# Moving weights laid with even columns first and read by TensorE from two halves in turn

## The chip, the core and the metric

The kernel runs on one core of one Trainium2 chip. The metric is device microseconds of one execution; lower is better. A core has five engines that run side by side, each with its own stream of instructions and synchronised by semaphores: TensorE (PE in the profile, with its weight loads as PEld), VectorE (DVE), ScalarE (ACT), GpSimd (POOL) and SyncE (SP), which here issues the transfers.

A matmul has two operands in on-chip memory (SBUF). The stationary one, 128 by 128, is loaded into the array first (LDWEIGHTS). The moving one is streamed past it, column by column: 128 partitions by up to 512 columns. In this kernel an activation block is stationary in some matmuls and a weight block in others; this change is about matmuls in which the *weight* is the moving operand.

## What is computed

A decoder trunk of two layers on 512 tokens with 1024 channels, all in float32. The parts that matter here, from the reference:

```python
def sq_relu_mlp(h, w_up, w_down):                      # both layers, d_ff = 4096
    u = jnp.matmul(h, w_up)
    return jnp.matmul(jnp.square(jax.nn.relu(u)), w_down)

for layer in range(2):
    h = rms_norm(x, mix_pre_g[layer])
    if layer < 1:
        m = pool_mixer(h, pool_w[layer], pool_scale[layer])
    else:
        q = jnp.matmul(h, w_q[0]) ...
        o = stick_breaking_attention(q, k, v)          # 16 heads of 64
        m = jnp.matmul(o..., w_o[0])
    x = x + rms_norm(m, mix_post_g[layer])
    h = rms_norm(x, mlp_pre_g[layer])
    x = x + rms_norm(sq_relu_mlp(h, w_up[layer], w_down[layer]), mlp_post_g[layer])
    if layer == 0:
        kv = jnp.matmul(rms_norm(x, kv_norm_g), w_kv)  # keys: first 1024 columns, values: last 1024
```

## The kernel before

Tokens lie in four blocks of 128 (`TS`), output channels in two blocks of 512 (`NS`). Float32 products are made from operands split into a high and a low part of type `fp32r`; a product is then three matmuls: high by high, high by low, low by high. The helper `mm3` (lines 317 to 320) emits these three for one pair of blocks, and its three lines carry them in the profile. Operands declared plain `F32` (the pooling mixer's products, line 872, and the scale row, line 802) aren't split by hand: one such matmul of the program shows as two rows in the trace.

Matmuls with the weight as the moving operand:

- `Seven.product`, line 625: the down projection of 28 of the 32 blocks of d_ff in each layer. Seven products stand for eight (a Strassen scheme over pairs of token halves and channel halves), in five groups of 2, 3, 3, 3 and 3 pairs of blocks. VectorE forms sums and differences of the weight's quarters (`right`, lines 592 to 611), ScalarE and VectorE split them into high and low parts (`split`, line 298), and the matmuls read them as `w[:, z, q]`, 512 columns at a time.
- `contract` (line 466), `finish` (line 480) and `projected` inside the attention's `end` (line 1187), all through `mm3`: the attention's output projection and the last four blocks of each down projection. In the last layer's last token block one 512 is cut into two of 256.
- `half_values` (line 941), through `mm3`: the values of the first eight heads, 512 columns wide. The values of the other heads (`values`, line 962) are 256 wide.

The up projection, queries and keys (`up_block`, lines 739 to 753, matmul lines 744, 747 and 748) have the weight stationary and the activations `xnh` and `xnl` moving.

Weights come from device memory by transfers that SP issues; the host lays each array out beforehand (in `kernel`, lines 1346 to 1387). Before the change the moving weights' columns lie in their natural order, so a moving operand of 512 columns is 512 neighbouring 4-byte words of each partition.

The order on each engine is partly written out by hand (`MIX_ORDER`, `ATT_ORDER`, `END_ORDER`, `MLP_ORDER`), and otherwise set by a planner.

Of the kernel before, what the change touches and what calls it, by code (L numbers as in the profile page):

```python
# [15 lines left out]
P = 128  # L16
D = 1024
S = 512
T = S // P
KC = D // P  # L20
FF = 4096
NJ = FF // P
# [6 lines left out]
PAIRS = HEADS // 2  # L29
# [2 lines left out]
TINY = 1e-24  # L32
TS = [slice(t * P, (t + 1) * P) for t in range(T)]
NS = [slice(0, 512), slice(512, 1024)]


SEG = {3: (0, 512), 2: (512, 384), 1: (896, 256), 0: (1152, 128)}
# [73 lines left out]
def trunk(ctx, tc, x, bands, grow, pw, wup, wdn, wq, wk, wv, wo, out):  # L111
# [16 lines left out]
    def ps():  # L128
        return psum.tile([P, 512], F32, tag="ps", name=name("ps"))
# [5 lines left out]
    ident, gc = eye[:, :P], eye[:, P:]  # L135
    for n in NS:
        nc.sync.dma_start(xt[0][:, n], x[TS[0], n])
# [7 lines left out]
    def xn_tile():  # L145
        turn[0] += 1
        return xn3[:, turn[0] % 3]
# [65 lines left out]
    apart, kept, going = [], {}, []  # L213
# [40 lines left out]
    def fill(n=1):  # L254
        if gate[0]:
            behind.update(latest)
        for _ in range(n):
            if queue and len(made) < ahead and (queue[0][0][0] != "dn" or dn_pool[0]):
                make()

    def get(key):
        while key not in made:
            make()
        return made.pop(key)

    for l in range(2):
        if l == 1:
            n = len(queue)
# [48 lines left out]
    def mm3(dst, ah, al, bh, bl, start, stop):  # L317
        nc.tensor.matmul(dst, ah, bh, start=start, stop=False)  # L318
        nc.tensor.matmul(dst, ah, bl, start=False, stop=False)  # L319
        nc.tensor.matmul(dst, al, bh, start=False, stop=stop)  # L320

    xnh = keep.tile([P, KC, S], F32R, tag="xnh", name="xnh")
    xnl = keep.tile([P, KC, S], F32R, tag="xnl", name="xnl")
# [6 lines left out]
    class Update:  # L330
        def __init__(self, t, gpost, scaled, eps=EPS, gpre=None, final=False, xn=None, gcol=None):
# [7 lines left out]

            self.cuts = NS  # L340
            if final and t == T - 1:
                self.cuts, self.scaled = [NS[0], slice(512, 768), slice(768, 1024)], xn_tile()

# [5 lines left out]
        def product(self, n, y, within=False):  # L349

            cut = self.cuts[n]
            if within:
                self.held[n] = y
            out = y if within else self.scaled[:, cut]
            return nc.vector.tensor_tensor(out=out, in0=y, in1=self.gpost[:, cut], op=ALU.mult)
# [110 lines left out]
    def contract(lhs, w, y, first, tiles):  # L466
        last = len(lhs) - 1
        for t in tiles:
            for n in NS:
                pd = ps()  # L470
                for c, ((lh, ll), (wh, wl)) in enumerate(zip(lhs, w)):
                    mm3(pd, lh[:, TS[t]], ll[:, TS[t]], wh[:, n], wl[:, n], c == 0, c == last)
                part = y[t][:, n]
                if first:
                    nc.scalar.copy(part, pd)
                else:
                    nc.vector.tensor_tensor(out=part, in0=pd, in1=part, op=ALU.add)
            fill()

    def finish(l, lhs, w, y, update):  # L480

        ups = [update(t, y[t]) for t in range(T)]
        bank, sums = {}, {}


        def within(t):
            return l == 1 and t >= T - 2

        def product(t, n, *cs):
            cut = ups[t].cuts[n]  # L490
            if (t, n) not in bank:
                bank[t, n] = ps()[:, : cut.stop - cut.start]
            for c in cs:
                (lh, ll), (wh, wl) = lhs[c], w[c]
                mm3(
                    bank[t, n], lh[:, TS[t]], ll[:, TS[t]], wh[:, cut], wl[:, cut], c == 0, c == len(lhs) - 1
                )

        def evacuate(t, n):
            part = y[t][:, ups[t].cuts[n]]  # L500
            src = bank.pop((t, n))
            total = sums[t, n] = src if within(t) else part
            nc.vector.tensor_tensor(out=total, in0=src, in1=part, op=ALU.add)

        def add(t, n, apart=False):
            (ups[t].add_apart if apart else ups[t].add_part)(n)
            if l == 1 and (t, n) != (T - 1, 1):
                cut = NS[1] if t == T - 1 and n == 2 else ups[t].cuts[n]
                nc.sync.dma_start(out[TS[t], cut], xt[t][:, cut])

        def transposes(t, h):
            bank["t", t, h] = ups[t].transposes(h)

        steps = {
            "p": product, "v": evacuate, "a": add, "t": transposes, "B": lambda: behind.update(latest),
            "s": lambda t, n: ups[t].squares_of(n, sums[t, n]), "A": lambda t, n: add(t, n, True),
            "g": lambda t, n: ups[t].product(n, sums[t, n], within(t)),
            "V": lambda t: ups[t].first_rstd(), "S": lambda t, n: ups[t].squares_of_x(n),
            "W": lambda t: ups[t].rstd(), "n": lambda t, n: ups[t].norm_part(NS[n]),
            "h": lambda t, h: ups[t].high(h, bank["t", t, h]), "l": lambda t, h: ups[t].low(h, bank["t", t, h]),  # L520
        }
        on = mybir.EngineType
        with tc.manual_schedule(engines={on.PE, on.Activation, on.DVE, on.Pool}):
            for step, which in MLP_ORDER[l]:
                steps[step](*which)
        if l == 0:
            for t in (T - 2, T - 1):
                pending[t] = ups[t]
# [4 lines left out]
    class Seven:  # L533
# [82 lines left out]
        def product(self, i, y, first):  # L616
            a, w = self.operands.pop(i)
            at, _, _, tokens, half = self.PRODUCTS[i]
            start = at not in self.banks
            if start:  # L620
                self.banks[at] = [ps(), ps()]
            for t, bank in enumerate(self.banks[at]):
                for q in range(self.n):
                    for k, (x, z) in enumerate(((0, 0), (0, 1), (1, 0))):
                        nc.tensor.matmul(  # L625
                            bank, a[:, x, q, TS[t]], w[:, z, q], start=start and q == 0 and k == 0,
                            stop=q == self.n - 1 and k == 2, skip_group_check=True,
                        )
                part = y[2 * tokens + t][:, NS[half]]
                if first and (tokens, half, t) not in first:  # L630
                    nc.scalar.copy(part, bank)
                    first.add((tokens, half, t))
                else:
                    nc.vector.tensor_tensor(out=part, in0=bank, in1=part, op=ALU.add)  # L634
# [291 lines left out]
    with tc.tile_pool(name="att", bufs=1, reuse_waits="tile") as ap:  # L926
        att_pool[0] = ap

        def value_tile(u):
            return ap.tile([P, T, 4, 2, HD], F32R, tag="v", bufs=2, name=name("v"))  # L930
# [8 lines left out]
        half_w, half_bank = [], {}  # L939

        def half_values(i, part):


            if not half_w:
                half_w.extend(get(("v", 0, h)) for h in range(4))
                for u in range(2):
                    vs[u] = None, value_tile(u)
            for s in part:
                if i == 0:
                    half_bank[s] = ps()  # L950
                for k in range(4 * i, 4 * i + 4):
                    (wh, wl), c = half_w[k // 2], NS[k % 2]
                    mm3(
                        half_bank[s], xnh[:, k, TS[s]], xnl[:, k, TS[s]], wh[:, c], wl[:, c], k == 0, k == KC - 1
                    )
                if i == 1:
                    for u in range(2):
                        value_parts(vs[u][1], s, half_bank[s][:, u * 256 : u * 256 + 256])
            if i == 1 and T - 1 in part:
                fill(ahead)  # L960
# [48 lines left out]
        with tc.issue_after(latest["pool"].ins):  # L1009
            nc.gpsimd.memset(begin, 0.0)  # L1010
            for lo, n in SEG.values():
                c = min(n - P, 1)
# [152 lines left out]
        def out_proj(u, tiles):  # L1165
            if u not in wos:
                wos[u] = [get(("o", 2 * u + c)) for c in range(2)]
            contract([os[2 * u + c] for c in range(2)], wos[u], y, u == 0, tiles)

        def end():  # L1170

            p, last = PAIRS - 2, PAIRS - 1
            heads[last] = [Head(qk[last], last, a) for a in range(2)]
            w = {c: get(("o", c)) for c in range(2, 6)}
            bank, o, ups, up, held = {}, {}, {}, {}, []
# [11 lines left out]
            def projected(key, t, n, pairs, first, stop):  # L1187
                if first:
                    bank[key, t, n] = ps()
                dst = bank[key, t, n]  # L1190
                for c in pairs:
                    (lh, ll), (wh, wl) = os[c], w[c]
                    mm3(
                        dst, lh[:, TS[t]], ll[:, TS[t]], wh[:, NS[n]], wl[:, NS[n]],
                        first and c == pairs[0], stop and c == pairs[-1],
                    )

# [190 lines left out]
```

## Time and profile before

| | |
|---|---|
| median of 3 runs | 945.31 us (943.88 to 946.74) |
| profiled execution | span 941.4 us from first to last instruction; the page gives no other time of that execution |
| TensorE busy | 932.5 us, 99% of the span, 4688 matmuls |
| VectorE, ScalarE, GpSimd busy | 695.8 us (74%), 559.6 us (59%), 41.0 us (4%) |
| granted TensorE clock | 0.999 of full speed, mean over the span |
| memory | 121.38 MB read, 33.55 MB written, mean 165 GB/s over the span |

The profile has one row for each instruction with its engine, source line, shapes, start and duration. Consecutive matmuls overlap: the next one starts while the last columns of the one before are still on their way out, so a matmul's *duration* is longer than what it costs in a dense stream. The cost is the distance from one start to the next, called its pace in what follows. The page's "busy" time of an engine counts overlapped stretches once.

### The profile page before, as it was taken

To read this page: it belongs to the slowest core of one execution; us is meant where nothing else is said; L and a number is where in the kernel's file an instruction comes from. 1 tells how busy PE (TensorE), PEld (TensorE's weight loads), DVE (VectorE), ACT (ScalarE), POOL (GpSimd) and SP (SyncE) were. 2 spreads that over 40 slices of the span, in tenths; PEclk is the share of its full clock that TensorE was granted. 3 is DMA by queue.
4 is the path that set the end of the run, shared out by engine and by line. 5 is a ranking of instruction groups with operands and counts; after the bars stand their busy time and mean duration, and the time that the engine had idled before them with its cause. 6 is when DMAs were issued, how large, how long until landed. Compare 5 with 4: busy or idle time off the path is not lost.

```text
span 941.4 us, 12325 instructions
## 1 busy us (share of the span) xinstructions
PE 932.5 (99%) x4688; PEld 787.6 (84%) x4688; DVE 695.8 (74%) x797; ACT 559.6 (59%) x986; POOL 41.0 (4%) x85
## 2 busy tenths in 40 slices
PE   9999999999999999999999999999999999999997
PEld 7988888888888888888889888898888888888886
DVE  5775898988979876178766388884696966958756
ACT  7568979788775546165545464875545444444532
POOL 3200000000000004000000001200000000000002
PEclk9999999999999999999999999999999999999999
DMA  8435959789697850633251361433414133133102
GB/s 302 163 106 186 333 200 375 291 284 343 223 325 281 276 192 2 223 134 134 84 178 53 120 261 45 153 139 100 169 45 156 68 134 112 45 135 112 34 11 90
DMA packets 42973, 155.73 MB, mean 165 GB/s; under 512 B 4257, under 2 KB 4385, under 8 KB 42914
## 3 DMA queue, kind: packets, MB, share of 16 engines
q1 hardware_dynamic: 42914, 154.95, 46.1%
q8 instruction: 37, 0.61, 0.3%
q14 instruction: 22, 0.18, 0.1%
HBM read 121.38 MB, written 33.55 MB: 165 GB/s over the span
## 4 chain that ended last, share of the span: by engine, by line
PE 97%; POOL 1%; ACT 1%; DVE 1%; DMA 0%; issue 0%; POOLq 0%; SPq 0%; ACTq 0%
PE ps L625 28%; PE ps L747 16%; PE ps L748 16%; PE ps L744 16%; PE ps L318 4%; PE ps L319 4%; PE ps L320 4%; PE ps L1093 2%; PE ps L1076 2%; PE ps L1118 2%; PE ps L872 1%; PE ps L425 1%; PE ps L844 1%; DMA x<-in_x 0%; ACT xn L303 0%
## 5 line engine op out<-in xcount | busy, mean ns | idle before, releaser
L625 PE MATMUL ps<-w,a 128*128 128x512 f32 x1176 | 278.6, 389 | 0.0
L747 PE MATMUL ps<-xnh,w 128*128 128x512 f32 (+1 forms) x704 | 260.5, 372 | 0.0
L748 PE MATMUL ps<-xnl,w 128*128 128x512 f32 (+1 forms) x704 | 259.8, 370 | 0.0
L625 PEld LDWEIGHTS ps<-w,a 128*128 128x128 f32 x1176 | 220.7, 188 | 45.9 <-DVE w L300 0.2
L744 PE MATMUL ps<-xnh,w 128*128 128x512 f32 (+1 forms) x704 | 259.0, 370 | 0.0
L744 PEld LDWEIGHTS ps<-xnh,w 128*128 128x128 f32 x704 | 132.2, 188 | 22.7
L748 PEld LDWEIGHTS ps<-xnl,w 128*128 128x128 f32 x704 | 132.7, 188 | 22.1
L747 PEld LDWEIGHTS ps<-xnh,w 128*128 128x128 f32 x704 | 132.2, 188 | 22.4
L634 DVE TENSOR_TENSOR y<-ps,y 128x512 f32<-128x512 f32 x124 | 84.4, 688 | 44.4 <-PE ps L625 44.2
L179 DVE TENSOR_TENSOR w<-raw,w 128x1024 fp32r<-128x1024 f32 x58 | 70.9, 1223 | 56.3 <-ACT w L177 56.1
L177 ACT CAST w<-raw 128x1024 fp32r<-128x1024 f32 x58 | 60.9, 1050 | 79.6 <-PE ps L744 78.3
L299 ACT CAST a<-r 128x768 fp32r<-128x768 f32 (+1 forms) x60 | 47.6, 794 | 72.5 <-PE ps L625 57.0
L300 DVE TENSOR_TENSOR a<-r,a 128x768 fp32r<-128x768 f32 (+1 forms) x60 | 54.1, 902 | 11.8 <-ACT a L299 11.6
L1057 DVE TENSOR_TENSOR_SCAN e<-u,begin 128x1280 f32<-128x1280 f32 x16 | 45.2, 2825 | 20.9 <-ACT u L1041 20.2
L299 ACT CAST w<-e 128x1536 fp32r<-128x1536 f32 (+1 forms) x30 | 41.8, 1393 | 23.1 <-DVE e L599 13.7
L300 DVE TENSOR_TENSOR w<-e,w 128x1536 fp32r<-128x1536 f32 (+1 forms) x30 | 49.4, 1648 | 1.9 <-ACT w L299 1.6
L189 ACT ACTIVATE apart<-apart,eye 128x128 f32<-128x128 f32 (+1 forms) x132 | 43.1, 405 | 0.3 <-DMA apart<-in_wk 0.3
L657 ACT ACTIVATE r<-ps 128x512 f32<-128x512 f32 x56 | 33.0, 590 | 8.7 <-PE ps L744 8.7
L300 DVE TENSOR_TENSOR w<-xn,w 128x1536 fp32r<-128x1536 f32 (+1 forms) x20 | 33.0, 1650 | 5.6 <-ACT w L299 5.5
L300 DVE TENSOR_TENSOR w<-w,w 128x1536 fp32r<-128x1536 f32 (+1 forms) x20 | 33.0, 1650 | 4.8 <-ACT w L299 4.8
L658 ACT ACTIVATE r<-r 128x512 f32<-128x512 f32 x56 | 35.5, 633 | 1.3
L307 POOL TENSOR_SCALAR stat<-stat,eps 128x1 f32<-128x1 f32 x8 | 5.4, 680 | 633.4 <-ACT xn L303 633.4
(140 smaller groups left out, 1330.7 us busy)
## 6 DMA issues: line engine op xcount, KB each, us to landing
raw<-in_wup SPq DMA_DIRECT2D x64, 512.0 KB, 4.2
w<-kept SPq DMA_DIRECT2D x60, 512.0 KB, 4.2
kept<-wx SPq DMA_DIRECT2D x30, 512.0 KB, 4.2
w<-in_wdn SPq DMA_DIRECT2D x8, 1536.0 KB, 6.9
kept<-apart SPq DMA_DIRECT2D x24, 512.0 KB, 6.1
xn<-in_wdn SPq DMA_DIRECT2D x8, 1536.0 KB, 7.5
apart<-in_wk SPq DMA_DIRECT2D x7, 512.0 KB, 7.1
apart<-in_wq SPq DMA_DIRECT2D x7, 512.0 KB, 9.3
```

The costliest lines, as they stand in the source:

```text
L177: nc.scalar.copy(hi, raw)
L179: nc.vector.tensor_tensor(out=lo, in0=raw, in1=hi.bitcast(F32), op=ALU.subtract)
L189: nc.scalar.mul(c, c, gc[:, at : at + 1])
L299: latest["act"] = nc.scalar.copy(hi, src)
L300: latest["dve"] = nc.vector.tensor_tensor(out=lo, in0=src, in1=hi.bitcast(F32), op=ALU.subtract)
L318: nc.tensor.matmul(dst, ah, bh, start=start, stop=False)
L625: nc.tensor.matmul(bank, a[:, x, q, TS[t]], w[:, z, q], start=start and q == 0 and k == 0, stop=q == self.n - 1 and k == 2, skip_group_che ...
L634: nc.vector.tensor_tensor(out=part, in0=bank, in1=part, op=ALU.add)
L744: nc.tensor.matmul(pu[:, cols], wl[:, k, :], xnh[:, k, cols], start=False, stop=k == KC - 1)
L747: nc.tensor.matmul(pu[:, cols], wh[:, k, :], xnh[:, k, cols], start=k == 0, stop=False)
L748: nc.tensor.matmul(pu[:, cols], wh[:, k, :], xnl[:, k, cols], start=False, stop=False)
L1057: nc.vector.tensor_tensor_scan(out=self.e[:, ::-1], data0=self.u[:, 1:][:, ::-1], data1=begin[:, ::-1], initial=0.0, op0=ALU.mult, op1=ALU ...
```

## The change

The host lays the columns of these weights out differently: in each block of 512 the 256 even columns come first, then the 256 odd ones (`apart`). The new function `woven` gives the matmul a view of that block which takes position 0, 256, 1, 257, 2, 258 and so on, which is the natural order of the columns again. So every output column stands where it stood. Two columns that follow each other in the stream lie 256 words (1024 bytes) apart in each partition.

The calls of `woven` are at all the places listed above: `Seven.product`, `contract`, `finish`, `half_values` and `projected`. The stationary operands, the outputs, the transfers' sizes, and all element-wise work on the weights (the sums of quarters, the split) are as before, the latter on columns in the new order. `values` and `up_block` are untouched.

```diff
+def woven(x, c):
+    h, n = c.start // S, S // 2
+    lo, hi = (c.start - h * S) // 2, (c.stop - h * S) // 2
+    return x[:, h * S : (h + 1) * S].rearrange("p (a b) -> p b a", a=2)[:, lo:hi]
...
 # contract
-    mm3(pd, lh[:, TS[t]], ll[:, TS[t]], wh[:, n], wl[:, n], c == 0, c == last)
+    mm3(pd, lh[:, TS[t]], ll[:, TS[t]], woven(wh, n), woven(wl, n), c == 0, c == last)
...
 # finish
-    bank[t, n], lh[:, TS[t]], ll[:, TS[t]], wh[:, cut], wl[:, cut], c == 0, c == len(lhs) - 1
+    bank[t, n], lh[:, TS[t]], ll[:, TS[t]], woven(wh, cut), woven(wl, cut), c == 0, c == len(lhs) - 1
...
 # Seven.product
-    bank, a[:, x, q, TS[t]], w[:, z, q], start=start and q == 0 and k == 0,
+    bank, a[:, x, q, TS[t]], woven(w[:, z, q], NS[0]), start=start and q == 0 and k == 0,
...
 # half_values
-    half_bank[s], xnh[:, k, TS[s]], xnl[:, k, TS[s]], wh[:, c], wl[:, c], k == 0, k == KC - 1
+    half_bank[s], xnh[:, k, TS[s]], xnl[:, k, TS[s]], woven(wh, c), woven(wl, c), k == 0, k == KC - 1
...
 # projected
-    dst, lh[:, TS[t]], ll[:, TS[t]], wh[:, NS[n]], wl[:, NS[n]],
+    dst, lh[:, TS[t]], ll[:, TS[t]], woven(wh, NS[n]), woven(wl, NS[n]),
...
 # kernel, on the host
+    apart = lambda w: w.reshape(*w.shape[:-1], -1, S // 2, 2).swapaxes(-1, -2).reshape(w.shape)
...
-        for w, n, c in ((a["w_kv"][:, D : D + 512], 512, 4), (a["w_kv"][:, D + 512 :], 256, 2))
+        for w, n, c in ((apart(a["w_kv"][:, D : D + 512]), 512, 4), (a["w_kv"][:, D + 512 :], 256, 2))
...
-        "wdn": a["w_down"].reshape(2, NJ, P, D),
+        "wdn": apart(a["w_down"]).reshape(2, NJ, P, D),
...
-        "wo": a["w_o"][0].reshape(PAIRS, P, D),
+        "wo": apart(a["w_o"][0]).reshape(PAIRS, P, D),
```

The change moves no instruction: on every engine the programs before and after have the same instructions in the same order, with the same shapes. Only the read pattern of the moving operands, and what the host puts at which address, differ. In the changed kernel every line number after line 35 is 8 higher (line 625 is 633 there, 318 is 326).

## The prediction

> **What bounds the kernel now.** I read the page first: span, busy shares, the slices, the chain that ended last.
>
> ```profile
> span 941.4 us, 12325 instructions
> PE 932.5 (99%) x4688; PEld 787.6 (84%) x4688; DVE 695.8 (74%) x797; ACT 559.6 (59%) x986; POOL 41.0 (4%) x85
> ...
> PE   9999999999999999999999999999999999999997
> ...
> PEclk9999999999999999999999999999999999999999
> ...
> PE 97%; POOL 1%; ACT 1%; DVE 1%; DMA 0%; issue 0%; POOLq 0%; SPq 0%; ACTq 0%
> ```
>
> TensorE is busy in every slice, at the full clock, and 97% of the chain that ended last runs through it. Busy doesn't mean that it couldn't be quicker, but it says that nothing else holds it up for long. The view of windows shows this by stage (columns: stretch, length, then busy time and count of PE, PEld, DVE, ACT and POOL, granted clock, DMA share, GB/s): the first MLP, then keys, values and attention, then the second MLP.
>
> ```profile
> 60.00:360.00 300.00, 300.00 (x1329) 248.49 (x1329) 248.02 (x256) 223.35 (x377) 4.91 (x9) 1.00 0.73 263
> 360.00:605.00 245.00, 244.84 (x1426) 210.07 (x1425) 163.03 (x202) 130.62 (x303) 14.56 (x34) 1.00 0.36 129
> 605.00:920.00 315.00, 315.00 (x1481) 264.65 (x1480) 227.32 (x247) 160.73 (x207) 1.16 (x3) 1.00 0.28 97
> ```
>
> Of these 860 us TensorE stands still for 0.16 us. Whatever is added to the pace of its matmuls in there is added to the time one for one, and a wait that would be shorter elsewhere gives nothing back. VectorE, the next engine, has 638 us of work in the same 860 us, and the change makes that slack larger, not smaller.
>
> **What one matmul costs.** The timeline of TensorE gives the pace (columns: start, length, instruction, count). Sixteen matmuls of line 625 stand in a row, and the next instruction starts at 203.99:
>
> ```profile
> 200.36 3.79 PE L625 MATMUL ps<-w,a 128*128 128x512 f32 x16
> 203.99 0.39 PE L744 MATMUL ps<-xnh,w 128*128 128x512 f32 x1
> ...
> 931.89 0.28 PE L318 MATMUL ps<-dn,sq 128*128 128x256 f32 x1
> ...
> 934.64 0.28 PE L320 MATMUL ps<-dn,sq 128*128 128x256 f32 x1
> ```
>
> (203.99 - 200.36) / 16 = 226.9 ns for 512 columns. The second pair is the first and the last of 24 matmuls of 256 columns in a row: (934.64 - 931.89) / 23 = 119.6 ns. So 256 columns cost 107.3 ns, 0.419 ns for a column, and each matmul has 226.9 - 214.6 = 12.3 ns that don't depend on its width.
>
> **The change, part by part.** Nothing is removed, added or moved: the instructions and their order are the same on every engine. The transfers carry the same bytes in the same shapes, and the element-wise work has the same shapes on permuted columns, so both are costed at nothing; their cover isn't needed. What changes is the address order in which a moving operand is read. Neighbours in the stream were 4 bytes apart, and are 1024 bytes apart now. Two things are needed: how many matmuls, and the new pace.
>
> The count, from line 625 and from the first line of the helper; its other two lines have the same numbers by the code, since each call emits the three together:
>
> ```profile
> L625 PE MATMUL ps<-w,a x1176: 389/389/389, 61.4 to 916.7; 128*128 128x512 f32 x196
> L318 PE MATMUL ps<-w,xnh x96: 277/283/476, 365.1 to 514.2; 128*128 128x256 f32 x64, 128*128 128x512 f32 x32
> L318 PE MATMUL ps<-dn,sq x68: 278/389/476, 337.9 to 934.4; 128*128 128x512 f32 x60, 128*128 128x256 f32 x8
> L318 PE MATMUL ps<-w,ohl x64: 388/394/481, 525.5 to 601.8; 128*128 128x512 f32 x64
> ```
>
> Of 512 columns: 1176 + 3 x (32 + 60 + 64) = 1644. (The form at the end of the first row is a sample; the count is x1176.) Of 256 columns: 3 x 8 = 24. The 64 of 256 columns in the second row are the values of the other heads, which aren't woven. At today's pace the 1644 take 373 us, two fifths of the time. All stand between 61 and 935 us.
>
> The pace of a woven matmul isn't in this trace: each moving operand here is a run of neighbouring words. So it is bounded from both sides. The nearest row below is today's pace, 226.9 ns: the order of the addresses doesn't matter. Below that I allow at most the width-independent 12.3 ns, since nothing in the trace streams a column in less than 0.419 ns, and I see no reason why jumps should take even those away. Above, the nearest rows are matmuls of the same size that run at half the rate, for another reason (plain F32 operands):
>
> ```profile
> L802 PE MATMUL ps<-row,ones x4: 592/592/593, 4.6 to 5.8; 128*128 128x512 f32 x4
> 4.55 1.88 PE L802 MATMUL ps<-row,ones 128*128 128x512 f32 x4
> L872 PE MATMUL ps<-pw,y x64: 379/379/410, 11.7 to 31.0; 128*128 128x256 f32 x64
> 11.82 6.92 PE ps L872 x32
> 4.00:7.00 3.00, 2.43 (x7) 0.84 (x4) 0.78 (x2) 1.51 (x5) 0.86 (x2) 1.00 0.98 292
> 11.60:18.80 7.20, 7.20 (x36) 6.28 (x36) 5.36 (x12) 5.04 (x14) 3.81 (x7) 1.00 1.02 393
> ```
>
> The four of line 802 lie (1.88 - 0.592) / 3 = 429 ns apart for 512 columns; line 872 needs 6.92 / 32 = 216 ns for 256 (a row of the chain, where overlaps are cut off). The last two rows show a granted clock of 1.00 around both, so this is not a slow clock: the array has a second pace, 0.84 ns for a column.
>
> I take the half rate: 429 ns for 512 columns, 216 for 256. The reason is the rate at which words must come in. At 0.419 ns for a column each partition delivers a 4-byte word every 0.419 ns. [...]
>
> ```profile
> L657 ACT ACTIVATE r<-ps 128x512 f32<-128x512 f32 x56 | 33.0, 590 | 8.7 <-PE ps L744 8.7
> L634 DVE TENSOR_TENSOR y<-ps,y 128x512 f32<-128x512 f32 x124 | 84.4, 688 | 44.4 <-PE ps L625 44.2
> ```
>
> ScalarE takes 590 / 512 = 1.15 ns for an element and VectorE 1.34, start included. A reader that is over twice as quick most likely gets neighbouring words in one fetch. If that is two words in a fetch every 0.84 ns, a woven stream, whose successive words are never neighbours, gets one useful word from each, which is the pace of line 802. This is an inference from rates, and the weakest step here.
>
> The sum against the profiled execution: 1644 x (429.3 - 226.9) ns = 332.7 us, and 24 x (216.3 - 119.6) ns = 2.3 us, 335.0 us together. The span goes from 941.4 to 1276.4 us. The median of the runs, 945.3, lies 3.9 us above that span; the same on top gives 1280 us. If the 12.3 ns stay beside the doubled stream (in line 802 they don't show), a woven matmul takes 441.5 ns, the sum is 1644 x 214.6 + 24 x 107.3 = 355 us, and the time 1300. If the last 2.3 us hide behind the tail of VectorE's additions it is 1278.
>
> [...]
>
> **The rivals.**
>
> Free reads, the other side (not slower): the array's feed takes one address for each column, or holds both runs at once, and the pace stays at 226.9 ns. The place is the same 1668 matmuls; the point that decides is whether a woven 512 starts its successor within 227 ns or not. Then nothing changes: 945 us. For it speaks that the pace splits so cleanly into a per-column part and 12.3 ns, with nothing that looks like a memory limit. Against it speaks the rate of words, above.
> [...]
>
> A fixed price: each woven matmul pays once more for its pattern, but streams at full pace. The nearest size for such a price is the 12.3 ns: 1668 x 12.3 ns = 20.5 us, 966 us.
>
> A quarter of the rate or less: a fetch brings four words and costs four columns' time, 858 ns for 512 and 429 for 256. That is 1644 x 631.5 + 24 x 309.6 ns = 1046 us more, 1991 us. No row of the trace has such a pace.
>
> A price in between: some jumps hidden, some not, anything from 966 to 1278 us.
>
> A gain: the 12.3 ns are a clash of neighbouring reads that jumps avoid, at most 20.5 us, 925 us. Nothing in the trace speaks for it.
>
> That the change doesn't do what it says: the two runs can't be merged into one run of neighbours, so the reads must jump. I give this no chance of its own.
>
> **How the numbers follow.** Chances: half rate 0.57, free 0.20, quarter rate or less 0.09, fixed price 0.08, in between 0.04, gain 0.02. The three runs shown lie within 0.15% of their median, so 0.3% (2.8 us) is about what can be told from no change. Faster: 0.02; same: the free case, 0.20; slower: the other four, 0.78. The likeliest case's own range is 1277 to 1301 us. The range for 8 in 10 must take in the free case, for without it and without the quarter rate too much is left out: 942 (945 less the bound) to 1301. It holds 0.57 + 0.20 + 0.08 + 0.04 = 0.89. Predicted: 1280 us.
>
> **What the profile after would show.** If right, the rows of line 633 (625 before) have a mean near 592 ns, as line 802 has, a start every 429 ns, and the same clock; the 512-wide rows of lines 326 to 328 the same, while lines 752, 755 and 756 (the up projection) stay at 389 ns. The MLP stages grow most, ScalarE and VectorE get longer idle times with PE as the releaser, and TensorE's busy share stays at 99%. If line 633 still has 389 ns, reads are free and I am wrong by the whole sum. If it has some 400 ns, it is the fixed price; above 900 ns, the quarter rate. If the untouched lines get slower too, something other than the read pattern acts, a lower granted clock first of all, and no step here covers that.

## The result: 1.4% faster, where 35% slower was forecast

The changed kernel takes 931.21 us (median of 4 runs, 929.77 to 933.46), the kernel before 944.60 us in the same comparison (943.50 to 946.74). The ratio is 0.9857, with a 95% interval of 0.9835 to 0.9879. The profiled execution is the longest of the four, 933.46 us with a span of 931.7 us.

The page of the changed kernel, the parts that answer to those shown of before (line numbers are 8 higher now):

```profile
span 931.7 us, 12325 instructions
PE 918.7 (99%) x4688; PEld 790.2 (85%) x4688; DVE 694.4 (75%) x797; ACT 558.9 (60%) x986; POOL 40.6 (4%) x85
...
PE 93%; DMA 2%; ACT 2%; DVE 1%; POOL 1%; issue 1%; SPq 0%; POOLq 0%; ACTq 0%; DVEq 0%
...
L633 PE MATMUL ps<-w,a 128*128 128x512 f32 x1176 | 265.9, 379 | 0.0
L755 PE MATMUL ps<-xnh,w 128*128 128x512 f32 (+1 forms) x704 | 261.6, 373 | 0.0
```

TensorE is as busy as before, but with less: 918.7 us in place of 932.5. The woven line has a mean length of 379 ns where it had 389; the up projection (line 755, 747 before) has 373 where it had 372. And the chain now has 2% of DMA and 2% of ScalarE in it, where TensorE alone held 97%. The timeline of TensorE shows the pace of line 633, and what stands right behind it:

```profile
198.76 3.19 PE L633 MATMUL ps<-w,a 128*128 128x512 f32 x14
201.78 0.40 PE L752 MATMUL ps<-xnh,w 128*128 128x512 f32 x1
202.02 0.39 PE L755 MATMUL ps<-xnh,w 128*128 128x512 f32 x1
...
203.85 0.39 PE L752 MATMUL ps<-xnh,w 128*128 128x512 f32 x1
204.08 0.39 PE L755 MATMUL ps<-xnh,w 128*128 128x512 f32 x1
```

(201.78 - 198.76) / 14 = 215.7 ns for a woven matmul, 11 ns less than before. The untouched rows behind it start 230 ns apart, (203.85 - 201.78) / 9, where 227 was the rule before, and the granted clock there is 1.00: the first ten or so neighbour-reading matmuls behind a woven run are a little slower than they were. That price wasn't in any case of the forecast, which named a lower clock as the first cause to look for if untouched lines got slower.

The stages (columns as in the prediction):

```profile
60.00:360.00 300.00, 297.30 (x1336) 251.40 (x1335) 247.11 (x256) 224.00 (x379) 5.78 (x10) 0.99 0.72 263
360.00:605.00 245.00, 243.97 (x1453) 213.12 (x1452) 165.50 (x207) 132.43 (x306) 14.38 (x34) 1.00 0.36 131
605.00:920.00 315.00, 315.00 (x1490) 269.61 (x1489) 231.84 (x255) 159.61 (x210) 3.39 (x5) 1.00 0.28 98
```

TensorE stands still for 2.7 us in the first stage, and the mean clock there is 0.99. Both belong to one place, near 341 us, and are taken up below.

### The profile page after: what moved, and what is told of

It reads as the page before. It is cut to its first block, busy times and chain, and to the rows that moved or that the text cites. A ratio compares the mean times of both kernels' runs of the same rounds, so it can differ in the third digit from the quotient of the medians.

```text
span 931.7 us, 12325 instructions
## 1 busy us (share of the span) xinstructions
PE 918.7 (99%) x4688; PEld 790.2 (85%) x4688; DVE 694.4 (75%) x797; ACT 558.9 (60%) x986; POOL 40.6 (4%) x85
## 4 chain that ended last, share of the span: by engine, by line
PE 93%; DMA 2%; ACT 2%; DVE 1%; POOL 1%; issue 1%; SPq 0%; POOLq 0%; ACTq 0%; DVEq 0%
PE ps L633 26%; PE ps L755 16%; PE ps L752 16%; PE ps L756 16%; PE ps L327 4%; PE ps L328 4%; PE ps L326 4%; PE ps L1101 2%; PE ps L1084 2%; PE ps L1126 2%; PE ps L880 1%; PE ps L433 1%; DMA kept<-apart 1%; PE ps L852 1%; DMA kept<-wx 1%
## 5 line engine op out<-in xcount | busy, mean ns | idle before, releaser
L633 PE MATMUL ps<-w,a 128*128 128x512 f32 x1176 | 265.9, 379 | 0.0
```

The source lines that it names most:

```text
L633: nc.tensor.matmul(bank, a[:, x, q, TS[t]], woven(w[:, z, q], NS[0]), start=start and q == 0 and k == 0, stop=q == self.n - 1 and k == 2, ...
```

## The experiments

In all of them a *pace* is the mean distance from the start of one matmul to the start of the next of its line, from the trace. A row's length in the groups of instructions is some 160 to 190 ns more. In the four kernels named `pat` only line 625's matmuls are changed, and each of the seven products of the Strassen scheme reads in another way, so that one profile holds seven cases; their outputs are permuted or meaningless columns, and their total times say nothing.

### Which ways of reading are faster (pat1, pat2)

The memory holds the columns in natural order; `m` is the moving operand of 512 neighbouring words, `a` the stationary one. Line numbers are those of the two profiles.

```diff
 # pat1
-    matmul(bank, a[:, x, q, TS[t]], w[:, z, q], ...)
+    629: m
+    631: m.rearrange("p (a b) -> p a b", a=2)[:, ::-1]          # halves swapped
+    633: m.rearrange("p (a b) -> p b a", a=2)                   # halves in turn
+    635: m.rearrange("p (b a) -> p a b", a=2)                   # all even, then all odd
+    637: m.rearrange("p (a b c) -> p b a c", a=2, c=4)          # halves in turn, 4 words each
+    639: m.rearrange("p (a b c) -> p b a c", a=2, c=2)          # halves in turn, 2 words each
+    641: m.rearrange("p (o a b) -> p o b a", a=2, b=2)          # 0 2 1 3, 4 6 5 7, ...
 # pat2
+    629: m
+    631: m.rearrange("p (a b) -> p b a", a=4)                   # four quarters in turn
+    633: m.rearrange("p (o a b) -> p o b a", a=2, b=4)          # 0 4 1 5 2 6 3 7, 8 12 ...
+    635: m.rearrange("p (o a b) -> p o b a", a=2, b=32)         # halves of each 64 in turn
+    637: m[:, ::-1]                                             # backwards
+    639: stationary a[:, x, q, t : S // 2 : 2], moving m
+    641: m.rearrange("p (b a) -> p b a", a=2)[:, :, ::-1]       # 1 0 3 2
```

> The kernel before, with columns in natural order in memory; line 625's matmuls read their moving operand in seven ways, one for each of the seven products, 168 matmuls each (outputs are then permuted columns, so only the pace counts). In order of lines: neighbours (control); the two halves swapped, each a run of 256 neighbours; halves in turn (the change's pattern); all even then all odd words (step 2); four words of one half, then four of the other; two and two; and 0,2,1,3 within each four words. Theory FORM: a moving pattern with more than one free dimension drops a fixed 11 ns, wherever the words lie: 227 ns for the control, 216 ns for the six others. Theory JUMP: reads of neighbouring words cost the 11 ns, by a clash in memory, and only successive words far apart avoid it: 227 for control, halves swapped, and 0,2,1,3; 216 for halves in turn; step 2 and the grains of 2 and 4 in between, 219 to 227.

> As the run before it, with seven other ways to read in line 625's matmuls, 168 each. In order of lines: neighbours (control); four quarters in turn; halves in turn within each 8 words (jumps of 16 bytes); halves in turn within each 64 words (jumps of 128 bytes); neighbours backwards (one dimension, step -1); the moving operand as before but the stationary one read with step 2 (every other token); and pairs swapped (1,0,3,2). Theory FORM: 227 for control, backwards, and the stationary one with step 2 (all have one free dimension in the moving operand), 216 for the four others. Theory JUMP: 216 for quarters and for 64 words; 227 for control, backwards, pairs swapped; 8 words in between. Theory CLASH WITH THE WEIGHT LOAD (moving reads collide with the stationary operand's): the stationary one with step 2 leaves 227, to 216 or to more than 235.

The groups by shape, first of pat1, then of pat2 (columns: line, engine, operands, count, busy us, mean length in ns, idle time before):

```profile
L635 PE MATMUL ps<-w,a 128*128 128x512 f32 x168 | 78.2, 630 | 0.0
L639 PE MATMUL ps<-w,a 128*128 128x512 f32 x168 | 58.7, 512 | 0.0
L637 PE MATMUL ps<-w,a 128*128 128x512 f32 x168 | 43.9, 416 | 0.0
L631 PE MATMUL ps<-w,a 128*128 128x512 f32 x168 | 40.7, 389 | 0.0
L629 PE MATMUL ps<-w,a 128*128 128x512 f32 x168 | 40.4, 389 | 0.0
L641 PE MATMUL ps<-w,a 128*128 128x512 f32 x168 | 40.1, 390 | 0.0
L633 PE MATMUL ps<-w,a 128*128 128x512 f32 x168 | 38.7, 379 | 0.0
```

```profile
L631 PE MATMUL ps<-w,a 128*128 128x512 f32 x168 | 49.7, 447 | 0.0
L637 PE MATMUL ps<-w,a 128*128 128x512 f32 x168 | 41.0, 398 | 0.0
L639 PE MATMUL ps<-w,a 128*128 128x512 f32 x168 | 40.8, 394 | 0.0
L629 PE MATMUL ps<-w,a 128*128 128x512 f32 x168 | 40.4, 389 | 0.0
L641 PE MATMUL ps<-w,a 128*128 128x512 f32 x168 | 40.1, 389 | 0.0
L633 PE MATMUL ps<-w,a 128*128 128x512 f32 x168 | 38.7, 379 | 0.0
L635 PE MATMUL ps<-w,a 128*128 128x512 f32 x168 | 38.4, 379 | 0.0
```

| order of the words | pace, ns |
|---|---|
| halves in turn; halves of each 64 in turn; halves of each 8 in turn | 216 |
| neighbours; halves swapped; 1 0 3 2; 0 2 1 3 | 227 |
| neighbours, stationary operand with step 2 | 233 |
| backwards | 234 |
| halves in turn, 4 words each | 251 |
| four quarters in turn | 280 |
| halves in turn, 2 words each | 339 |
| all even, then all odd (step 2) | 452 |

FORM falls: halves swapped, 1 0 3 2 and 0 2 1 3 are patterns of several dimensions and take 227 ns, and other such patterns are far slower (251 to 339 ns). JUMP falls too: jumps of 16 bytes (0 4 1 5) do as well as jumps of 1024 bytes (216 ns both), and a plain step of 8 bytes is the worst of all (452 ns). CLASH WITH THE WEIGHT LOAD forecast 216 or more than 235 for the stationary operand with step 2; its 233 is neither. The half pace that the prediction took for the woven read exists, and it belongs to step 2.

What orders most of the table is a model of the author's. Let the words lie in lines of four (16 bytes), and let the even places of the stream be read by one reader and the odd places by another. In the 216 ns rows each reader takes four words from a line, one after the other; in the 227 ns rows two; with step 2 one (0, 4, 8 for one reader, 2, 6, 10 for the other). The rows in which a reader goes back and forth between lines (2 words each, 4 words each, quarters) lie in between and aren't explained by that count alone. Nor is the read backwards: it takes two words of a line for each reader, and its pace is 234 ns, not 227. No row shows a line itself; that it holds 16 bytes is an estimate from these rows. With lines of 8 bytes each reader would take one word of a line for neighbours and two for 0 2 1 3, but both have 227 ns; with lines of 32 bytes it would take four both for neighbours and for 0 4 1 5, but these have 227 and 216 ns.

### Testing that account (pat3, pat4)

```diff
 # pat3; two = 1024 neighbouring words, zeros = a bf16 tile of zeros
+    632: stationary with step 2, moving halves in turn
+    634: two.rearrange("p a (b c) -> p b a c", c=2)[..., 0]     # two runs in turn, each step 2
+    636: 64 stationary columns, moving m
+    638: zeros[:, ::4]                                          # bf16, step 4, 256 columns
+    640: 32 stationary columns, moving m
+    642: zeros[:, :512]                                         # bf16, neighbours
+    644: two.rearrange("p a (b c) -> p b a c", c=4)[..., 0]     # two runs in turn, step 4, 256 columns
 # pat4
+    633, 635: of each three matmuls two with halves in turn, the middle one m
+    637: m.rearrange("p (a b c) -> p b a c", a=2, c=8)          # halves in turn, 8 words each
+    639: halves in turn, 256 columns
+    641: zeros[:, ::2]                                          # bf16, step 2, 512 columns
+    643: m[:, :128]
+    645: two[:, 2:514]                                          # neighbours from the middle of a line
+    647: halves in turn, 128 columns
```

> The kernel before, with seven other operands in line 625's matmuls, 168 each (the outputs lose their meaning; only the pace counts). Theory LINES AND LOAD: even and odd places of the stream are read by two readers out of 16-byte lines; a reader that takes 4 words of each line has fetches to spare, one that takes 2 has none, one that takes 1 is at half pace; the weight load's own lines then add the 11 ns when nothing is spare. Theory SAME LINE: two successive words in one line clash, whatever the weight load does. In order of lines: halves in turn and the stationary operand with step 2: 216 by the first theory (spare fetches take up the weight load), 222 to 233 if the longer weight load costs by itself. Two runs in turn, each with step 2: 227 by the first, 216 by SAME LINE. Neighbours with 64 of 128 stationary columns: 221 by the first, 227 by SAME LINE. bf16, step 4, 256 columns: 226 or more by the first (1 word of a line for each reader), 112 to 120 if only 4-byte words matter. Neighbours with 32 stationary columns: 219 by the first, 227 by SAME LINE. bf16 neighbours: 216 by the first (4 words of a line for each reader), 227 by SAME LINE. Two runs in turn with step 4, 256 columns: 226 or more by the first, 110 by SAME LINE.

> The kernel before, with seven other operands in line 625's matmuls (the outputs lose their meaning; only the pace counts). Theory LINES: each of two readers (even and odd places of the stream) takes words from 16-byte lines; 4 words of a line for each reader give 216 ns for 512 columns, 2 give 227, 1 half pace. [...] Product 0, of each three matmuls the middle one with neighbours, the others in turn: 216 and 227 if each matmul stands for itself; 234 for the lone one if a change of pattern costs more, as the first rows behind a woven run in the changed kernel had. Product 1, 8 words of one half, then 8 of the other: 227 plus half of what grains of 4 cost more (251 - 227), 239, if each jump between runs costs by itself. Product 2, in turn with 256 columns: 112, as in the run of all at once. [...] Product 4, neighbours with 128 columns: 65 if the 11 ns are fixed, 56 to 62 if they shrink with width. Product 5, neighbours from the middle of a line: 227; more if the first line counts. Product 6, in turn with 128 columns: 54 to 58.

The groups of pat3, then those of pat4:

```profile
L634 PE MATMUL ps<-w,a 128*128 128x512 f32 x168 | 41.3, 391 | 3.1 <-ACT a L299 3.1
L636 PE MATMUL ps<-w,a 128*64 128x512 f32 x168 | 40.9, 392 | 0.0
L644 PE MATMUL ps<-w,a 128*128 128x256 f32 x168 | 40.9, 415 | 0.0
L640 PE MATMUL ps<-w,a 128*32 128x512 f32 x168 | 40.7, 394 | 0.0
L638 PE MATMUL ps<-zeros 128*128 128x256 bf16 x168 | 39.7, 405 | 0.0
L632 PE MATMUL ps<-w,a 128*128 128x512 f32 x168 | 38.7, 380 | 0.0
L642 PE MATMUL ps<-zeros 128*128 128x512 bf16 x158 | 35.7, 379 | 0.7
```

```profile
L637 PE MATMUL ps<-w,a 128*128 128x512 f32 x168 | 45.0, 414 | 4.7 <-ACT a L299 4.7
L645 PE MATMUL ps<-w,a 128*128 128x512 f32 x168 | 41.1, 397 | 0.0
L641 PE MATMUL ps<-zeros 128*128 128x512 bf16 x158 | 39.2, 388 | 0.7
L635 PE MATMUL ps<-w,a 128*128 128x512 f32 x56 | 22.5, 402 | 0.0
L639 PE MATMUL ps<-w,a 128*128 128x256 f32 x168 | 21.5, 276 | 0.0
L647 PE MATMUL ps<-w,a 128*128 128x128 f32 x168 | 20.1, 272 | 0.0
L643 PE MATMUL ps<-w,a 128*128 128x128 f32 x168 | 20.0, 272 | 0.0
```

Paces here are medians, since some rows also hold a wait or a stretch at half clock.

| operands | words of a line for each reader | forecast with LINES | pace, ns |
|---|---|---|---|
| bf16 neighbours | 4 | 216 | 216 |
| halves in turn, stationary with step 2 | 4 | 216 | 216 |
| bf16 with step 2 | 2 | 227 if the weight load plays no part | 226 |
| two runs in turn, each step 2 | 2 | 227 | 227 |
| bf16 with step 4, 256 columns | 1 | 226 or more | 227 |
| two runs in turn, each step 4, 256 columns | 1 | 226 or more | 228 |
| halves in turn, 256 columns | 4 | 112, taken from the run `best` | 112 |

SAME LINE falls: in the two runs of step 2 successive words never share a line, and the pace is still 227 ns. The count of words for each reader forecast five of these rows, for 4-byte and for 2-byte words; for bf16 with step 2 it gave 227 on a condition, and the last row was read off an earlier run. It remains a model: no row shows the readers or the lines themselves, and it leaves the rows named above without a cause.

Do the 11 ns hang on the weight load? With 64 and 32 stationary columns the pace is 230 and 232 ns, where LINES AND LOAD forecast 221 and 219. And bf16, whose weight loads have rows of 96 ns here where those of fp32r have some 190, has 226 ns at two words of a line; if the 11 ns went with the length of those rows, it would be some 222 (an estimate: 216 + 11 x 96 / 190). The stationary operand with step 2 costs 6 ns where the moving one has neighbours and nothing where it is woven. So how the stationary operand lies matters a little, and only in some rows, but its load isn't the source. That they belong to the start of the matmul itself would fit these rows; no run shows it.

Three misses: 8 words of each half in turn take 242 to 245 ns, not 239; neighbours from the middle of a line take 235, where 227 was forecast, or more if the first line counts; and 128 columns take 111 ns woven or not, where 54 to 65 were forecast. Since 256 woven columns also take 112 ns, where 0.419 ns for a column gives 107, matmuls of this kind in a row seem not to start oftener than every 112 ns. The trace of pat4 points at the weight load: nearly everywhere the first matmul of 128 columns in a row is followed after only 55 to 58 ns, while all later ones stand some 111 ns apart, and the weight loads of these rows start 112 ns apart too. No run varied the load alone at this width, so this stays likely and not shown. A lone neighbour-reading matmul between woven ones has a median of 231 ns, between the 227 and the 234 that were forecast.

### The two parts of the change alone (sevenonly, restonly)

```diff
 # sevenonly: woven and apart only for line 625 and its 28 blocks of each w_down
 # restonly:  woven and apart only for the other places
-    bank, a[:, x, q, TS[t]], woven(w[:, z, q], NS[0]), ...
+    bank, a[:, x, q, TS[t]], w[:, z, q], ...
```

> Only line 625's 1176 matmuls are read in turn (the down projection's first 28 blocks); output projection, values and last blocks stay with neighbours. If the gain is 11 ns for each woven matmul and all of it reaches the end: 1176 x 11 = 12.9 us, 932 us. If the wait of 3 us at 338 us in the changed kernel (the last down blocks wait for a transfer, then some matmuls run at half clock, some 5 us in all) comes from line 625 being earlier, it shows here too: 937 us. If it comes from the woven values or output projection it is gone: 932 us.

> The other part of the change alone: output projection, values of the first eight heads and the last four down blocks are read in turn (468 matmuls of 512 columns and 24 of 256), line 625 with neighbours. If 11 ns for each reach the end: 468 x 11 = 5.2 us and 0.2 us, 939 us. If first rows of neighbours behind a woven run cost more, as in the changed kernel (about 45 ns for each change), there are few such places here: still 939. If the last down blocks of the first layer now wait for their transfer (2.7 us and matmuls at half clock behind it): 942 to 943. With line 625 alone (9.8 us) the two should add up to the change's 13.4 us, less what the wait takes.

Line 625 alone: 934.46 us against 944.28, ratio 0.9899 (0.9874 to 0.9923). The rest alone: 940.14 us against 945.16, ratio 0.9951 (0.9934 to 0.9967). The drops, 1.0% and 0.5%, add up to 1.5%, and the whole change gave 1.4%. So both kinds of places gain: 9.8 us for 1176 matmuls and 5.0 us for 492. The first gained less than the 12.9 us of the forecast, and its trace shows where the rest went: line 625 takes 12.7 us less, and all untouched lines together 2.9 us more, most of it (2.6 us) in the up projection's rows behind woven runs, as in the changed kernel. Neither profile has the long wait near 341 us; as the next section shows that it differs from run to run, one profile of each can't say which part brings it. The profile of restonly is of its slowest execution, 942.62 us where the other three took 940.14 or less: TensorE stands still for 2.59 us near 12 us, ahead of every woven matmul, and then has a clock of 0.50 for 3.4 us.

### The wait near 341 us (again1, again2, afterR)

In the profiled execution of the changed kernel, VectorE waits for a transfer to finish writing out a tile before it may overwrite it, and TensorE waits for VectorE (timeline, then a window of TensorE with its clock):

```profile
339.84 1.23 DVE L187 TENSOR_TENSOR dn<-dn,dn 128x1024 fp32r<-128x1024 f32 x1 [3.63 <-DMA kept<-apart]
341.12 0.48 PE L327 MATMUL ps<-dn,sq 128*128 128x512 f32 x1 [2.70 <-DVE dn L187]
...
342.81 0.63 PE L327 MATMUL ps<-dn,sq 128*128 128x512 f32 x1
343.24 0.63 PE L328 MATMUL ps<-dn,sq 128*128 128x512 f32 x1
...
342.40:345.60 3.20, 3.20 (x9) 0.50 0.34 109
```

After 2.70 us without work, and 1.1 us after work resumed, the granted clock falls to 0.50 for 3.4 us: starts are 427 ns apart. Stops of 2.59 us in restonly, 2.28 us in moreA (near 332 us) and 2.18 us in pat3 (near 12 us) each had 3.4 us at 0.50 behind them too. Of three stops of 2.35 us, the two in pat4 (near 236 and 296 us) brought the half clock and the one in pat3 (near 247 us) didn't, so the length of the stop alone doesn't decide it. How much of the gain went there was open, so the changed kernel was profiled twice more.

> The changed kernel once more, for the wait at 341 us. Its profiled execution took 933.46 us, the longest of four (929.77 the shortest). If the wait of 2.7 us and the half clock behind it (4.2 us together) differ from run to run, a run near 930 has a gap under 1 us there and no pace of 427 ns, and a run near 933 has both. If they stand in each run, both appear in a run near 930 too, and the spread of 3.7 us has another source.

> The same again, since one more profile may fall on either side: the gap before the last down blocks of the first layer (near 341 us), against the execution's time. With the wait 932 to 934 us, without it 929 to 931, if the wait is what makes the spread; no such order if not.

The rows at the same place, again1 (930.23 us) first, then again2 (929.16 us):

```profile
338.32 1.23 DVE L187 TENSOR_TENSOR dn<-dn,dn 128x1024 fp32r<-128x1024 f32 x1 [1.89 <-DMA kept<-apart]
339.60 0.48 PE L327 MATMUL ps<-dn,sq 128*128 128x512 f32 x1 [0.96 <-DVE dn L187]
```

```profile
336.00 1.22 DVE L187 TENSOR_TENSOR dn<-dn,dn 128x1024 fp32r<-128x1024 f32 x1
...
341.06 0.48 PE L327 MATMUL ps<-dn,sq 128*128 128x512 f32 x1 [0.19 <-DVE dn L187]
```

The wait is 2.70, 0.96 and 0.19 us, and the times are 933.46, 930.23 and 929.16: it differs from run to run with the landing of the transfers, and goes with the spread of the times in these three. The half clock came with the longest wait only.

A kernel with other memory for these blocks was to take the wait away:

```diff
-    c, d = (piece("apart", 1, 3)[:, 0] for _ in range(2))
+    free = piece("r", 3, 2)
+    c, d = free[:, 0], free[:, 1]
+    dn_raw["dn", l, NJ - 1] = xn_tile()
```

> The changed kernel, with other memory for the last down blocks of each layer: the third block's parts go to the space of the squares instead of the tile that a transfer still writes out, and the fourth block's raw weights to a free third of xn3, so that their transfer needn't wait for a buffer. If the wait of 2.7 us at 341 us and the matmuls at half clock behind it (7 x 0.21 us) are where part of the gain went: 927 to 928 us, no gap over 0.3 us there, and no pace of 427 ns. If the transfers themselves are late (the queue is full there) the wait moves by a block and the time stays at 931.

It takes 930.26 us (928.98 to 933.36), ratio 0.9856 (0.9838 to 0.9873): no gain over the changed kernel that can be told, as the second case has it. Its profile has a wait of 0.78 us for the next block, whose transfer landed late by itself (in the changed kernel's profile the DMA engines are 85% busy from 325 to 341 us):

```profile
340.72 1.04 ACT L185 CAST dn<-xn 128x1024 fp32r<-128x1024 f32 x1 [5.56 <-DMA xn<-in_wdn]
...
343.07 0.48 PE L327 MATMUL ps<-dn,sq 128*128 128x512 f32 x1 [0.78 <-DVE dn L187]
```

### The activations in turn as well (moreA, best)

If the pattern counts and not the weights, the up projection, queries and keys must gain too. There the activations move. They are read in turn from their natural order, so the result's columns are permuted, and the engines that take it from PSUM put them back with step 2:

```diff
 # up_block
-    nc.tensor.matmul(pu[:, cols], wh[:, k, :], xnh[:, k, cols], ...)
+    nc.tensor.matmul(pu[:, cols], wh[:, k, :], in_turn(xnh[:, k, cols]), ...)
 # up
-    nc.scalar.activation(r, pu, ACT.Relu)
+    nc.scalar.activation(as_order(r, parts), in_order(pu, parts), ACT.Relu)
+    # in_turn:  x.rearrange("p (a b) -> p b a", a=2)
+    # in_order: pu.rearrange("p (h b a) -> p h a b", h=parts, a=2)
```

> The changed kernel, and also the activations that are moving in the up projection, queries and keys are read halves in turn (tokens t and t+256 in turn); ScalarE and VectorE put the columns back in order when they read the result with step 2 from PSUM. 1728 matmuls of 512 and 384 of 256 columns change. If the pace falls by 11 ns for any operand that is read in turn: 2112 x 11 ns = 23 us less TensorE work than in the changed kernel, 908 us if nothing else becomes late, some 912 to 920 with new waits. If the gain belongs to weights or to the data that is read and not to the pattern: 931 us, and lines of the up projection stay at 389 ns. If reading PSUM with step 2 makes ScalarE's relu (590 ns) twice as long, 56 x 0.6 = 33 us more ScalarE work, which has 40% slack: hidden, at most 5 us shown.

It takes 909.50 us (908.40 to 910.73) against 944.28, ratio 0.9631 (0.9608 to 0.9653): a further 22 us below the changed kernel's 931.2, where 23 less new waits was forecast. The up projection's rows, 373 ns long in the changed kernel (line 755), have lost the same 11 ns as the weights' rows (line 765 here), so the pattern counts and not the weights, and the Relu on ScalarE takes 590 ns as before. Some of the gain was lost to a wait at the last down blocks, with a clock of 0.50 for 3.4 us behind it:

```profile
L765 PE MATMUL ps<-xnh,w 128*128 128x512 f32 (+1 forms) x704 | 253.4, 362 | 0.0
L666 ACT ACTIVATE r<-ps 128x512 f32<-128x512 f32 x56 | 33.1, 590 | 4.4 <-PE ps L762 4.4
332.41 0.48 PE L327 MATMUL ps<-dn,sq 128*128 128x512 f32 x1 [2.28 <-DVE dn L187]
```

The last kernel adds afterR's memory, and reads the remaining values (192 matmuls of 256 columns) in turn:

> All at once: weights and activations in turn, the other memory for the last down blocks, and the values of the other heads (192 matmuls of 256 columns) in turn as well. From 909.5 us: the wait at 332 us and the half clock behind it (2.3 + 7 x 0.21 = 3.7 us) and 192 x 10 ns = 1.9 us fall away, 904 us. If the transfers are late by themselves, 907.6 us.

It takes 906.81 us (905.43 to 907.93) against 944.07, ratio 0.9603 (0.9590 to 0.9617), the fastest of all. That lies between the two cases, nearer to late transfers: its profile still has a wait of 0.78 us at the last down blocks, but no half clock behind it, and the remaining values start 112 ns apart where they started 120 ns apart before. Its page and its timeline:

```profile
span 904.4 us, 12347 instructions
PE 892.5 (99%) x4688; PEld 787.0 (87%) x4688; DVE 693.0 (77%) x797; ACT 557.6 (62%) x986; POOL 40.9 (5%) x85
...
690.33 4.05 PE L633 MATMUL ps<-w,a 128*128 128x512 f32 x18
694.22 0.38 PE L767 MATMUL ps<-xnh,w 128*128 128x512 f32 x1
...
696.80 0.38 PE L767 MATMUL ps<-xnh,w 128*128 128x512 f32 x1
```

The up projection's rows start 215 ns apart right behind the woven run, (696.80 - 694.22) / 12: with one pattern on both the price of a change of pattern is gone too.

## Why the prediction was wrong, step by step

**What bounds the kernel: right.** The order of instructions didn't change, TensorE bound the kernel at every stage, and what its woven matmuls saved came out at the end, less the dearer rows behind them and some waits.

**The count: right.** 1644 matmuls of 512 columns and 24 of 256 are read in turn, as counted.

**The pace of a woven matmul: wrong, and here the forecast failed.** It took the half rate, 429 ns, from the upper bound; the chip took 215.7. The inference was that a quick reader fetches two neighbouring words at once, so that a woven stream wastes half of each fetch. The runs show the opposite order: no read of 4-byte words that was tried is faster than the woven one, and step 2 has the half rate (452 ns). How many words of a line the even and the odd places take orders most of the rows; that it is the cause is a model. The rows cited for it, line 802 and line 872, are slow for another reason, as the text itself said; that the array has a pace of 0.84 ns for a column said nothing about which pattern meets it. Nor did the rates of ScalarE and VectorE.

**The lower bound: right in size, wrong in weight.** The case called a gain had the size of what happened: at most the 12.3 ns that don't depend on the width, 925 us. The measured 11.0 ns for 1644 matmuls and some 8 for 24 are 18.3 us. The text gave it 2 in 100 because it saw no reason for it. But the trace had shown that each matmul took 12 ns more than its columns, an unexplained cost at the very place that the change touches, and that deserved an experiment in thought: something in how these matmuls read might remove it.

**What the order of the words does: not in the forecast.** The prediction asked only whether words that follow each other in the stream are neighbours in memory. In the runs that doesn't set the pace: of two orders that jump at each word, 0 4 1 5 has 216 ns and step 2 has 452, and neighbours lie between them with 227. In the model of 16-byte lines, 0 4 1 5 changes the line at each word, and step 2 takes two words of each line, one after the other. So a count over the whole stream doesn't fit the runs; a count of words of a line for every other word fits the rows of the second table, but not the quarters (280 ns), the grains of 2, 4 and 8 words (339, 251 and 242 to 245 ns) or the read backwards (234 ns).

**What the prediction didn't have: the part given back.** 18.3 us of saved pace became 13.4 in the medians. In again2's trace against that of before (span 927.4 against 941.4) the distances from each woven row to the next row are 17.3 us less in sum, and all others 3.1 us more. Between 18.3 and 17.3 stand mostly waits right behind woven rows: 0.7 us for ScalarE at 580 us, behind the output projection, where it was 0.2 before, and 0.2 us at the last down blocks. Of the 3.1 us, 2.7 are the up projection's rows behind woven runs in the two MLPs. In the execution of 933.46 us the wait near 341 us and the half clock behind it took 4.2 us more than in again2.

**What stays open:** why the in-between patterns (quarters, 2, 4 and 8 words, backwards) cost what they do, what the 11 ns at two words of a line are made of, why a change of pattern takes ten matmuls to settle, and what besides the length of a stop halves the clock.

## What to carry to other kernels

Where TensorE is the bound, compare the pace of its matmuls with their columns: a cost that doesn't scale with the width (12.3 of 226.9 ns before the change) is a question about how operands are read or loaded, and one profile with a different pattern on each line answers it at the price of a single run. For 4-byte moving operands, reading two runs in turn, one word each, took 216 ns for 512 columns in place of 227; it is worth having on all matmuls or on long stretches of them (a change back to neighbours cost some 39 ns here, 2.7 us over 69 changes, as much as four woven matmuls save), and step 2 (452 ns) is to be avoided. Where the nearest row in a trace is slow for another reason, it bounds a cost but doesn't say which end is likely.

## What the runs showed of the hardware that was not expected

- A moving operand of 512 4-byte words: 216 ns with two runs in turn, also when the two are only 16 bytes apart; 227 for neighbours; 452 with step 2.
- 2-byte words: 216 ns for neighbours, 226 with step 2, and 227 for 256 columns with step 4, in the order that the model's count of words from a 16-byte line gives.
- Matmuls of 256 woven columns and of 128 columns in a row start every 111 to 112 ns; in pat4 nearly every first one of 128 columns behind a wider one is followed sooner, after 55 to 58 ns.
- The first ten neighbour-reading matmuls behind a woven run took up to 240 ns, 231 in the mean, then 227 again.
- The granted clock fell to 0.50 at stops of TensorE of 2.18 to 2.70 us in five profiles, for 3.4 us each time, but not at one of 2.35 us in pat3; behind gaps of 0.96 us and less near 341 us no matmul had the pace of 427 ns.
